# An encoder trunk on one core: the order at the start of a feed-forward stage, the place of a bias table's loads, and a last block turned back in two parts

## The chip, the core and the metric

The kernel runs on one core of a Trainium2 chip. Its engines each work through a queue of their own, in order: TensorE (PE: matmuls and transposes, with PEld for loading weights), VectorE (DVE), ScalarE (ACT), GpSimd (POOL), and SyncE (SP), which only issues DMAs. POOL issues DMAs too: those that add what they load to what is there. An instruction waits on semaphores for what it needs from other engines, and all that stands behind it in its queue waits with it.

The metric is the time of one execution in microseconds (us) on the device. One execution was also recorded by the profiler; the tables and rows come from it.

## The reference

A bidirectional encoder of two layers over 512 tokens of width 1024, all in float32. Each layer has a half-weighted SwiGLU feed-forward stage, a mixer, a second feed-forward stage, and a gated embedding (DEPTH is 2, the feed-forward width 2816):

```python
for i in range(DEPTH):
    h = h + 0.5 * swiglu(rmsnorm(h, norm_ffn1[i]), ffn1_w_gate[i], ffn1_w_up[i], ffn1_w_down[i])
    hn = rmsnorm(h, norm_mix[i])
    if i % 2 == 0:
        h = h + ab_mixer(hn, w_in_ab[j], sink_a[j], w_out_ab[j], pos)
    else:
        h = h + c_mixer(hn, w_in_c[j], rpb_c[j], w_out_c[j])
    h = h + 0.5 * swiglu(rmsnorm(h, norm_ffn2[i]), ffn2_w_gate[i], ffn2_w_up[i], ffn2_w_down[i])
    gate = jax.nn.sigmoid(rmsnorm(h, norm_ple[i]) @ w_ple_gate[i])
    h = h + gate * (p[i] @ w_ple_proj[i])
return rmsnorm(h, norm_final)

def swiglu(x, w_gate, w_up, w_down):
    return (jax.nn.silu(x @ w_gate) * (x @ w_up)) @ w_down
```

`c_mixer`, the mixer of the second layer, is a neighbourhood attention that adds a learned bias for each head and each offset in row and column, `rpb_c`.

## The kernel before

**Products.** A float32 operand is split into a high part, which ACT rounds off (L154), and the rest, which DVE subtracts (L155). Each product is three matmuls of these parts: high by high, high by low, low by high. So every weight that arrives passes ACT and then DVE before PE can use it. `wr` and `tmp` are raw weights, `wh` and `wl` their parts; `act` are activations and their parts.

**A feed-forward stage** (`ffn`) runs four times: two layers, two stages in each. It has four steps.
- `front` computes the first columns of gate and up as plain products over eight chunks of the input, into four PSUM banks, two called `mm` and two called `sc`. Meanwhile it computes the norm of each token (`stat`): PE sums up the squares, DVE makes the mean `ms` (L237), POOL raises it to the power -1/2 as `rcol` (L238). At the end DVE makes `minus`, which is minus `rcol` (L283), ACT applies Silu from each bank (L291) and DVE multiplies gate and up (L292), which reads the bank too. In the last four chunks, `halves` (L301 to L311) makes sums and differences of the input's quarters, for the blocks.
- `block` runs five times. Each multiplies a tile of 2 by 2 quarters by a scheme with seven products in place of eight, of 24 matmuls each. Its quarters of weights, q0 to q3, come in two ways: `whole` loads two units of 512 KB into `wr` on SP's queue (L329), and `add` lets a DMA on POOL's queue add another quarter to them (L335); `pieces` loads four units of 256 KB into `tmp` (L341), to which POOL's queue may add four more (L343). The first product uses the pieces of q3; the second uses `whole(q0)`, writes the `sc` banks, and thus waits until L291 and L292 have read what `front` left there; the third uses `whole(q2)`, the fourth the pieces of q1 and q2. L392 adds one whole quarter to another on DVE.
- `between` and `turn_back` transpose each block's result so that it can be the next operand: sixteen transposes of 128x128 on PE (L425), in groups of four into one bank, and one eviction by ACT for each group (L426). For the first four blocks this happens within the next block. For the last one, `turn` does it in `down`.
- `down` multiplies by the third matrix. It works in units of two chunks: `first(s)` splits the left halves of the activations (`x1`) and multiplies, `second(s)` splits the right ones (`x2`) and multiplies, `fifth` and the others follow. `turn()` is called once, behind `second(0)`; `first(1)` and `second(1)` come right behind it and split the two pairs of activations that `turn` appended. The four turns are at about 249, 880, 1273 and 1841 us.

**Order.** The code is written in one stream, and a scheduler orders each engine's queue from it, by what every step needs and by priorities: work inside `tc.high_priority()` goes first. `issue_after(x)` tells the scheduler to queue what is in it behind instruction x. The rest of the order comes out of the scheduler: which load stands before which on SP, or which split before which on DVE, is nowhere written out.

**Bias table.** `c` (the second layer's mixer) regroups `rpb` into a table in DRAM, `rpb_u`, by 32 DMAs of 15 KB from DRAM to DRAM (L1222). They depend on nothing, and the scheduler put them at the start of the program; the first reader runs at about 1404 us.

Of the kernel before, what the change touches and what calls it, by code (L numbers as in the profile page):

```python
# [13 lines left out]
ALU = mybir.AluOpType  # L14
# [42 lines left out]
class Trunk:  # L57
# [172 lines left out]
    def stat(self, tag, cols):  # L230
# [7 lines left out]
        nc.gpsimd.tensor_tensor(r[:, :n], ms[:, :n], self.mhalf[:, :n], op=ALU.pow)  # L238
# [27 lines left out]
    def front(self, w):  # L266
# [18 lines left out]
        for b in (2, 3, 0, 1):  # L285
# [4 lines left out]
            with self.tc.high_priority():  # L290
                nc.scalar.activation(g, banks[b][:, :M // 2], AF.Silu, scale=r)  # L291
                nc.vector.scalar_tensor_tensor(out[b], banks[b][:, M // 2:], r, g, op0=ALU.mult, op1=ALU.mult)  # L292
# [21 lines left out]
    def block(self, w, y, t, between, late):  # L314
# [10 lines left out]
        def whole(q):  # L325
            out = []
            for u in range(2):
                raw = self.wr.tile([P, UNIT], F32, tag="wr", name=self.nm("wr"))
                nc.sync.dma_start(raw, q[:, u * UNIT:(u + 1) * UNIT])  # L329
                out.append(raw)  # L330
# [6 lines left out]
        def pieces(q, more=None):  # L337
            out = []
            for k in range(half):
                raw = self.tmp()  # L340
                nc.sync.dma_start(raw, q[:, k * M:(k + 1) * M])  # L341
# [31 lines left out]
        chain = whole(q0)  # L373
# [8 lines left out]
        product(A, base, y[:half], l, True, False)  # L382
# [4 lines left out]
        product(C, pieces(q1, q2), t34, l, True, True)  # L387
# [31 lines left out]
    def turn_back(self, rows, bank):  # L419

        out = []
        for c in range(rows[0].shape[-1] // P):
# [7 lines left out]
    def ffn(self, i, which, k_next):  # L430
# [23 lines left out]
        for j in range(BLOCKS):  # L454
            n = 4 * UNIT + j * 8 * UNIT
            rows = self.block(gu[:, n:n + 8 * UNIT], y, t, between, late)
        self.begin_norm(k_next)
        p = lambda: [self.per_layer(i, c) for c in range(2)]
        self.down(dn, a, xs, sums, begin, kept, p if which == 2 else None, lambda: a.extend(self.turn_back(rows, self.sbank)))
# [16 lines left out]
    def down(self, w, a, xs, sums, begin, kept, inner, turn):  # L476
# [108 lines left out]
        for s in range(n):  # L585
            first(s)
            second(s)
            if s == 0:
                turn()
                r3 = [self.sbank(), self.sbank()]  # L590
# [610 lines left out]
    def c(self, k_next):  # L1201
# [15 lines left out]
        pad = io["rpb"]  # L1217
        nr = 2 * NA_KH - 1
        ud = self.dp.tile([NA_KW, 16, 2, nr, 16], F32, name="rpb_u")
        for c in range(NA_KW):  # L1220
            for g in range(2):
                nc.sync.dma_start(ud[c, :, g], bass.AP(tensor=pad.tensor, offset=pad.offset + NA_KW - 1 - c + 16 * g,  # L1222
                                                       ap=[[nr * RPB_W, 16], [RPB_W, nr], [1, 16]]))
        uh = ud.rearrange("c h g d r -> c (h g) (d r)")
# [65 lines left out]
        self.out_proj(io["o_c"], mix, KC - 2, k_next, self.kept)  # L1290

# [167 lines left out]
def encoder_trunk(ctx: ExitStack, tc: tile.TileContext, io: dict):  # L1459
    t = Trunk(ctx, tc, io)  # L1460
    t.setup()
    for i in range(DEPTH):
        t.ffn(i, 1, 4 * i + 1)
# [145 lines left out]
```

## Time and profile before

| | |
|---|---|
| time, median of three runs | 2020.44 us (2017.29, 2020.44, 2022.22) |
| time of the profiled execution | 2017.92 us |
| its span, first to last instruction | 2016.2 us |
| mean granted clock of TensorE | 0.996 of full speed |
| busy ACT | 1214.6 us (60% of the span), 2059 instructions |
| busy POOL | 342.3 us (17%), 398 instructions |
| read from HBM | 313.86 MB, 164 GB/s over the span |

The profile is one execution on the chip. A row of an engine in order of time gives the start in us from the span's start, the busy time, the engine, the line of the code, the operation with what it writes and reads, and how many like instructions in a row it holds; in brackets stands the time that the engine stood idle ahead of it, and what released it. PE's, DVE's and ACT's times are those of the engine's work; DMA issues on SP (SPq) give how long the queue was held. A stretch row gives the stretch, its length, then busy time of PE, PEld, DVE, ACT and POOL, the granted clock, the DMA share (over 1 when transfers queue up) and GB/s. The profile's span is what the engines worked; the time has 1.72 us around it.

### The profile page before, as it was taken

The page shows a single profiled execution, that of the slowest core. Times are in us where ns is not written, and L with a number is a line of the kernel's source. Part 1 is how long each engine was busy: PE and PEld are TensorE (multiplying, and loading weights), DVE is VectorE, ACT ScalarE, POOL GpSimd, SP SyncE. Part 2 cuts the span into 40 slices and gives each one's busy share as a digit, 9 for nine tenths or more (in the row PEclk, how much of TensorE's full clock was granted, in tenths as well). Part 3 has the DMA queues.
Part 4 walks back from the last instruction along what each step waited for, and adds up shares of the span by engine and source line. Part 5 has one row for each costly group of instructions (what it writes and reads, how often), then busy time and mean ns, then how long its engine had stood idle before and what let it go on. Part 6 is the DMA issues. An engine that isn't in the chain of part 4 may idle for free. (4 is left out here: it accounts for less than half of the span.)

```text
span 2016.2 us, 28073 instructions
## 1 busy us (share of the span) xinstructions
PE 1983.2 (98%) x9750; PEld 1652.0 (82%) x9750; DVE 1513.0 (75%) x2600; ACT 1214.6 (60%) x2059; POOL 342.3 (17%) x398
## 2 busy tenths in 40 slices
PE   8999999999999999999999999999999999999998
PEld 6888888878888888878888888788888888887886
DVE  7677876798766677786787678857887767778675
ACT  6655665477645665665566656745766566666553
POOL 1211011342211221112122120111000122111211
PEclk9999999999999999999999999999999999999999
DMA  9877687644335887779578786885343487776971
GB/s 271 185 194 184 151 198 202 185 94 85 89 74 186 194 195 174 173 177 213 195 229 183 169 186 174 191 195 183 105 131 106 161 205 185 170 172 177 216 229 43
DMA packets 150495, 344.05 MB, mean 171 GB/s; under 512 B 26320, under 2 KB 34000, under 8 KB 150352
## 3 DMA queue, kind: packets, MB, share of 16 engines
q1 hardware_dynamic: 109248, 227.89, 35.0%
q0 software_dynamic: 40960, 114.32, 32.3%
q8 instruction: 77, 1.26, 0.3%
q14 instruction: 66, 0.54, 0.1%
q10 hardware_dynamic: 144, 0.04, 0.0%
HBM read 313.86 MB, written 17.27 MB: 164 GB/s over the span
## 5 line engine op out<-in xcount | busy, mean ns | idle before, releaser
L154 ACT ACTIVATE wh<-wr 128x1024 fp32r<-128x1024 f32 (+1 forms) x408 | 419.1, 1029 | 434.0 <-PE mm L367 92.7
L155 DVE TENSOR_TENSOR wl<-wr,wh 128x1024 fp32r<-128x1024 f32 (+1 forms) x408 | 486.8, 1195 | 250.7 <-ACT wh L154 247.8
L365 PE MATMUL mm<-wh,act 128*128 128x512 f32 x640 | 250.7, 392 | 0.0
L367 PE MATMUL mm<-wh,act 128*128 128x512 f32 x640 | 250.6, 392 | 0.0
L366 PE MATMUL mm<-wl,act 128*128 128x512 f32 x640 | 249.3, 389 | 0.0
L154 ACT ACTIVATE wh<-tmp 128x512 fp32r<-128x512 f32 x280 | 165.7, 625 | 107.8 <-PE sc L367 32.7
L155 DVE TENSOR_TENSOR wl<-tmp,wh 128x512 fp32r<-128x512 f32 x280 | 181.8, 683 | 21.2 <-ACT wh L154 20.3
L179 PE MATMUL mm<-act,wh 128*128 128x512 f32 (+1 forms) x472 | 184.8, 393 | 0.4 <-ACT act L154 0.4
L181 PE MATMUL mm<-act,wl 128*128 128x512 f32 (+1 forms) x472 | 184.2, 391 | 0.0
L180 PE MATMUL mm<-act,wh 128*128 128x512 f32 (+1 forms) x472 | 184.1, 391 | 0.0
L335 POOL DMA_DIRECT2D wr<-in_gu_dram x80 | 78.8, 986 | 397.7 <-DVE wl L155 361.2
L366 PEld LDWEIGHTS mm<-wl,act 128*128 128x128 f32 x640 | 120.2, 188 | 24.5
L367 PEld LDWEIGHTS mm<-wh,act 128*128 128x128 f32 x640 | 120.2, 188 | 24.3
L365 PEld LDWEIGHTS mm<-wh,act 128*128 128x128 f32 x640 | 120.2, 188 | 23.7
L155 DVE TENSOR_TENSOR act<-act,act 128x512 fp32r<-128x512 f32 (+1 forms) x208 | 128.2, 638 | 9.5 <-ACT act L154 8.7
L365 PE MATMUL sc<-wh,act 128*128 128x512 f32 x320 | 125.4, 392 | 8.2 <-DVE act L292 8.2
L154 ACT ACTIVATE act<-act 128x512 fp32r<-128x512 f32 (+1 forms) x208 | 116.1, 588 | 26.9 <-PE sc L518 9.4
L508 POOL DMA_DIRECT2D wr<-in_dn_dram x80 | 69.4, 882 | 363.1 <-DVE wl L155 211.2
L367 PE MATMUL sc<-wh,act 128*128 128x512 f32 x320 | 125.3, 392 | 0.0
L366 PE MATMUL sc<-wl,act 128*128 128x512 f32 x320 | 125.2, 391 | 0.0
L343 POOL DMA_DIRECT2D tmp<-in_gu_dram x80 | 71.7, 1043 | 289.6 <-DVE act L473 134.3
L517 PE MATMUL mm<-wh,act 128*128 128x512 f32 x248 | 97.7, 394 | 5.4 <-ACT act L154 5.4
(271 smaller groups left out, 4562.3 us busy)
## 6 DMA issues: line engine op xcount, KB each, us to landing
wr<-in_gu_dram SPq DMA_DIRECT2D x92, 512.0 KB, 4.9
tmp<-in_gu_dram SPq DMA_DIRECT2D x160, 256.0 KB, 3.8
wr<-in_gu_dram POOLq DMA_DIRECT2D x80, 512.0 KB, 7.5
wr<-in_dn_dram POOLq DMA_DIRECT2D x64, 512.0 KB, 7.5
tmp<-in_dn_dram SPq DMA_DIRECT2D x120, 256.0 KB, 4.1
tmp<-in_gu_dram POOLq DMA_DIRECT2D x80, 256.0 KB, 5.9
wr<-in_dn_dram SPq DMA_DIRECT2D x32, 512.0 KB, 4.9
act<-kept SPq DMA_DIRECT2D x56, 256.0 KB, 4.6
```

The costliest lines, as they stand in the source:

```text
L154: self.put(self.nc.scalar.activation(hi, src, AF.Copy))
L155: self.put((lo_eng or self.nc.vector).tensor_tensor(lo, src, hi.bitcast(F32), op=ALU.subtract))
L179: mm(out, stat[0], mov[0], start=start, stop=False)
L180: mm(out, stat[0], mov[1], start=False, stop=False)
L181: return mm(out, stat[1], mov[0], start=False, stop=stop)
L335: nc.gpsimd.dma_start(raw, q[:, u * UNIT:(u + 1) * UNIT], accum_op=ALU.add)
L343: nc.gpsimd.dma_start(raw, more[:, k * M:(k + 1) * M], accum_op=ALU.add)
L365: mm(p, xh, wh, start=start and k == 0, stop=False, skip_group_check=True)
L366: mm(p, xh, wl, start=False, stop=False, skip_group_check=True)
L367: self.last_mm = mm(p, xl, wh, start=False, stop=stop and k == half - 1, skip_group_check=True)
L508: nc.gpsimd.dma_start(raw, b[:, u.start * T:u.stop * T], accum_op=ALU.add)
L517: mm(p, xh, wh, start=start and k == 0, stop=False, skip_group_check=True)
```

## The change

Four things change.

1. *The start of each feed-forward stage.* In every first to fifth block, the pieces of q1 and q2 and the DMAs that add to them are queued behind the last `power` (L238) that was issued. In the very first block of the program alone (`start`), two more: the loads of q0 are queued behind the last piece of q3 (`last_piece`), and the third product, with its splits, behind the last Silu of `front` (`last_silu`).
2. *The bias table* leaves `c` and becomes a function of its own, `bias_table`, called ahead of the second layer. Its DMAs are queued behind the last whole load (`last_load`) that was issued by then, which is one of the last block of the first layer's second feed-forward stage.
3. *The last block's turn* is made in two calls: the first two groups of four transposes behind `second(0)` as before, the other two behind `first(1)`.
4. `turn_back` takes the groups that it is to turn, and the Silu's, power's and loads' instructions are kept in names so that others can be queued behind them.

What is computed is the same.

```diff
+        self.power = nc.gpsimd.tensor_tensor(r[:, :n], ms[:, :n], self.mhalf[:, :n], op=ALU.pow)
...
+                self.last_silu = nc.scalar.activation(g, banks[b][:, :M // 2], AF.Silu, scale=r)
...
-    def block(self, w, y, t, between, late):
+    def block(self, w, y, t, between, late, start):
...
+                self.last_load = nc.sync.dma_start(raw, q[:, u * UNIT:(u + 1) * UNIT])
...
+                self.last_piece = nc.sync.dma_start(raw, q[:, k * M:(k + 1) * M])
...
         product(B, pieces(q3), y[half:], l, True, True)
-        chain = whole(q0)
+        with self.tc.issue_after(self.last_piece.ins) if start else ExitStack():
+            chain = whole(q0)
...
         base = whole(q2)
-        product(A, base, y[:half], l, True, False)
+        with self.tc.issue_after(self.last_silu.ins) if start else ExitStack():
+            product(A, base, y[:half], l, True, False)
...
-        product(C, pieces(q1, q2), t34, l, True, True)
+        with self.tc.issue_after(self.power.ins):
+            mixed = pieces(q1, q2)
+        product(C, mixed, t34, l, True, True)
...
-    def turn_back(self, rows, bank):
+    def turn_back(self, rows, bank, cs=None):
...
-        for c in range(rows[0].shape[-1] // P):
+        for c in cs or range(rows[0].shape[-1] // P):
...
-            rows = self.block(gu[:, n:n + 8 * UNIT], y, t, between, late)
+            rows = self.block(gu[:, n:n + 8 * UNIT], y, t, between, late, first and j == 0)
...
-        self.down(dn, a, xs, sums, begin, kept, p if which == 2 else None, lambda: a.extend(self.turn_back(rows, self.sbank)))
+        self.down(dn, a, xs, sums, begin, kept, p if which == 2 else None, lambda n: a.extend(self.turn_back(rows, self.sbank, n)))
...
         for s in range(n):
             first(s)
+            if s == 1:
+                turn(range(2, 4))
+                r3 = [self.sbank(), self.sbank()]
             second(s)
             if s == 0:
-                turn()
-                r3 = [self.sbank(), self.sbank()]
+                turn(range(2))
...
+    def bias_table(self):
...
+        with self.tc.issue_after(self.last_load.ins):
+            for c, g in ((c, g) for c in range(NA_KW) for g in range(2)):
+                self.nc.sync.dma_start(self.ud[c, :, g], bass.AP(tensor=pad.tensor, offset=pad.offset + NA_KW - 1 - c + 16 * g,
+                                                       ap=[[nr * RPB_W, 16], [RPB_W, nr], [1, 16]]))
...
     for i in range(DEPTH):
+        if i % 2:
+            t.bias_table()
         t.ffn(i, 1, 4 * i + 1)
```

How this moves the queues shows at three places. The rows give the line, the operation, what it writes and reads, and the shape; the lines of the new kernel are some higher (L380 was L379, L396 was L392, L430 was L426).

SP's queue at the start of the program, behind the loads of the input and of `front`'s weights. `ident` and `sink` are small constants, `wr` the whole quarters q0 (473, 475) and q2 (529, 531), `tmp` 429 to 435 the pieces of q3. Before:

```order
L147 DMA ident<-in_ident_dram 128x128
L329 DMA wr_473<-in_gu_dram 128x1024
L329 DMA wr_475<-in_gu_dram 128x1024
L907 DMA sink_3269<-in_sink_dram 128x12
L1222 DMA rpb_u<-in_rpb_dram 16x15x16 x2
L329 DMA wr_529<-in_gu_dram 128x1024
L1222 DMA rpb_u<-in_rpb_dram 16x15x16 x3
L329 DMA wr_531<-in_gu_dram 128x1024
L1222 DMA rpb_u<-in_rpb_dram 16x15x16
L341 DMA tmp_429<-in_gu_dram 128x512
L341 DMA tmp_431<-in_gu_dram 128x512
```

Now:

```order
L147 DMA ident<-in_ident_dram 128x128
L913 DMA sink_3269<-in_sink_dram 128x12
L341 DMA tmp_429<-in_gu_dram 128x512
L341 DMA tmp_431<-in_gu_dram 128x512
L341 DMA tmp_433<-in_gu_dram 128x512
L341 DMA tmp_435<-in_gu_dram 128x512
L329 DMA wr_473<-in_gu_dram 128x1024
L329 DMA wr_475<-in_gu_dram 128x1024
L329 DMA wr_529<-in_gu_dram 128x1024
L329 DMA wr_531<-in_gu_dram 128x1024
```

The four pieces of q3 moved from behind four whole loads and six DMAs of the table to a place ahead of all of them; the table is gone from here. It is now in the same queue in the last block of the first layer's second feed-forward stage, in groups of 6, 15, 1 and 10 between the loads of `down`'s weights.

DVE's queue from `minus` to the first L292, the multiplication that frees the `sc` banks. `wl_534` and `wl_538` are splits of q2, `wr_529` under L392 the sum of two quarters. Before:

```order
L283 TENSOR_SCALAR minus_403<-rcol_322 128x4
L155 TENSOR_TENSOR act_370<-act_360,act_369 128x512
L155 TENSOR_TENSOR wl_534<-wr_529,wh_533 128x1024
L308 TENSOR_TENSOR act_389<-act_385 128x256
L310 TENSOR_TENSOR act_390<-act_387,act_385 128x256
L309 SCALAR_TENSOR_TENSOR act_389<-act_389,act_387 128x256
L392 TENSOR_TENSOR wr_529<-wr_529,wr_473 128x1024
L311 SCALAR_TENSOR_TENSOR act_390<-act_389,act_387 128x256
L155 TENSOR_TENSOR act_396<-act_389,act_395 128x512
L155 TENSOR_TENSOR wl_538<-wr_531,wh_537 128x1024
L155 TENSOR_TENSOR act_400<-act_390,act_399 128x512
L292 SCALAR_TENSOR_TENSOR act_405<-sc_224,rcol_322,act_406 128x256
```

Now the same stretch, up to the first row behind the four L292:

```order
L155 TENSOR_TENSOR act_370<-act_360,act_369 128x512
L308 TENSOR_TENSOR act_389<-act_385 128x256
L309 SCALAR_TENSOR_TENSOR act_389<-act_389,act_387 128x256
L310 TENSOR_TENSOR act_390<-act_387,act_385 128x256
L311 SCALAR_TENSOR_TENSOR act_390<-act_389,act_387 128x256
L155 TENSOR_TENSOR act_396<-act_389,act_395 128x512
L155 TENSOR_TENSOR act_400<-act_390,act_399 128x512
L292 SCALAR_TENSOR_TENSOR act_405<-sc_224,rcol_322,act_406 128x256
L292 SCALAR_TENSOR_TENSOR act_405<-sc_225,rcol_322,act_406 128x256
L292 SCALAR_TENSOR_TENSOR act_411<-mm_222,rcol_322,act_412 128x256
L292 SCALAR_TENSOR_TENSOR act_411<-mm_223,rcol_322,act_412 128x256
L155 TENSOR_TENSOR wl_534<-wr_529,wh_533 128x1024
```

The two splits and the sum of quarters that stood ahead of L292 stand behind it. `minus` has left this stretch as well; it now stands further ahead, between the last L311 of the second half and the split of the fourth piece of q3:

```order
L308 TENSOR_TENSOR act_329<-act_325 128x256
L237 TENSOR_SCALAR ms_321<-tr_316 128x4
L309 SCALAR_TENSOR_TENSOR act_329<-act_329,act_327 128x256
L310 TENSOR_TENSOR act_330<-act_327,act_325 128x256
L311 SCALAR_TENSOR_TENSOR act_330<-act_329,act_327 128x256
L283 TENSOR_SCALAR minus_403<-rcol_322 128x4
L155 TENSOR_TENSOR wl_444<-tmp_435,wh_443 128x512
L155 TENSOR_TENSOR act_336<-act_329,act_335 128x512
```

It reads `rcol`, which POOL's L238 writes; in POOL's queue the power stood behind one adding DMA in the first block and now stands ahead of it. In the first blocks of the three other feed-forward stages three to six adding DMAs change places with the power in the same way.

ACT's queue at the first turn. `act_2236` to `act_2257` (before) and `act_2236` to `act_2284` (now) are the evictions of the four groups of transposes, the rows with `act_1192`, `act_1522`, `act_1199` and `act_1529` are the splits of the activations for `first(1)` and `second(1)`, `wh_2361` the split of a weight. Before:

```order
L154 ACTIVATE wh_2361<-tmp_2363 128x512
L426 ACTIVATE act_2236<-sc_2235 128x512
L426 ACTIVATE act_2243<-sc_2242 128x512
L154 ACTIVATE wh_2361<-tmp_2364 128x512
L426 ACTIVATE act_2250<-sc_2249 128x512
L426 ACTIVATE act_2257<-sc_2256 128x512
L154 ACTIVATE act_2267<-act_1192 128x512
L154 ACTIVATE act_2271<-act_1522 128x512
L154 ACTIVATE act_2292<-act_1199 128x512
```

Now:

```order
L154 ACTIVATE wh_2361<-tmp_2363 128x512
L430 ACTIVATE act_2236<-sc_2235 128x512
L430 ACTIVATE act_2243<-sc_2242 128x512
L154 ACTIVATE act_2251<-act_1192 128x512
L154 ACTIVATE wh_2361<-tmp_2364 128x512
L154 ACTIVATE act_2255<-act_1522 128x512
L430 ACTIVATE act_2277<-sc_2276 128x512
L430 ACTIVATE act_2284<-sc_2283 128x512
L154 ACTIVATE act_2292<-act_1199 128x512
```

The split of `act_1192`, which the first product behind the turn needs, stood behind all four evictions and stands behind two now. On PE nothing changes places: the sixteen transposes still follow each other, and the products of `first(1)` come behind them.

More of the change, by code (lines that the diff above doesn't have):

```diff
@@ L237, in stat @@
         nc.vector.tensor_scalar(ms[:, :n], ps[:, :n], 1.0 / D, EPS, op0=ALU.mult, op1=ALU.add)
-        nc.gpsimd.tensor_tensor(r[:, :n], ms[:, :n], self.mhalf[:, :n], op=ALU.pow)
+        self.power = nc.gpsimd.tensor_tensor(r[:, :n], ms[:, :n], self.mhalf[:, :n], op=ALU.pow)
         return r
@@ L290, in front @@
             with self.tc.high_priority():
-                nc.scalar.activation(g, banks[b][:, :M // 2], AF.Silu, scale=r)
+                self.last_silu = nc.scalar.activation(g, banks[b][:, :M // 2], AF.Silu, scale=r)
                 nc.vector.scalar_tensor_tensor(out[b], banks[b][:, M // 2:], r, g, op0=ALU.mult, op1=ALU.mult)
@@ L328, in whole @@
                 raw = self.wr.tile([P, UNIT], F32, tag="wr", name=self.nm("wr"))
-                nc.sync.dma_start(raw, q[:, u * UNIT:(u + 1) * UNIT])
+                self.last_load = nc.sync.dma_start(raw, q[:, u * UNIT:(u + 1) * UNIT])
                 out.append(raw)
@@ L340, in pieces @@
                 raw = self.tmp()
-                nc.sync.dma_start(raw, q[:, k * M:(k + 1) * M])
+                self.last_piece = nc.sync.dma_start(raw, q[:, k * M:(k + 1) * M])
                 if more is not None:
@@ L1215, in constants @@
                         nc.scalar.activation(dst[i][hf][free, :], t[free, :], AF.Copy)
[L1217 to L1224, printed above, removed]
+        uh = self.ud.rearrange("c h g d r -> c (h g) (d r)")
         nat = lambda x, b: x[:, b * P:(b + 1) * P]
@@ L1290, in c @@
         self.out_proj(io["o_c"], mix, KC - 2, k_next, self.kept)
+    def bias_table(self):
+        pad = self.io["rpb"]
+        nr = 2 * NA_KH - 1
+        self.ud = self.dp.tile([NA_KW, 16, 2, nr, 16], F32, name="rpb_u")
+        with self.tc.issue_after(self.last_load.ins):
+            for c, g in ((c, g) for c in range(NA_KW) for g in range(2)):
+                self.nc.sync.dma_start(self.ud[c, :, g], bass.AP(tensor=pad.tensor, offset=pad.offset + NA_KW - 1 - c + 16 * g,
+                                                       ap=[[nr * RPB_W, 16], [RPB_W, nr], [1, 16]]))
     @staticmethod
```

## The prediction

> **What bounds the kernel now.** I read the page's first part, then the busy time in stretches of 20 us, then the order of time of each engine where a stretch is not full.
>
> ```profile
> PE 1983.2 (98%) x9750; PEld 1652.0 (82%) x9750; DVE 1513.0 (75%) x2600; ACT 1214.6 (60%) x2059; POOL 342.3 (17%) x398
> ...
> 20.00:40.00 20.00, 14.24 (x67) 11.59 (x65) 17.73 (x36) 14.18 (x22) 8.72 (x9) 0.99 1.08 303
> 40.00:60.00 20.00, 17.58 (x73) 14.52 (x74) 10.90 (x16) 11.10 (x20) 3.56 (x5) 0.84 0.94 168
> ...
> 240.00:260.00 20.00, 18.26 (x88) 14.84 (x87) 16.80 (x27) 14.42 (x25) 2.60 (x3) 1.00 0.70 164
> ...
> 880.00:900.00 20.00, 18.26 (x86) 14.67 (x85) 17.42 (x30) 16.16 (x28) 2.32 (x3) 1.00 0.82 190
> ...
> 1260.00:1280.00 20.00, 18.26 (x88) 14.87 (x87) 18.14 (x30) 15.04 (x26) 2.59 (x3) 1.00 0.74 175
> ...
> 1840.00:1860.00 20.00, 18.26 (x81) 14.50 (x80) 15.29 (x26) 14.64 (x25) 2.60 (x3) 0.91 0.75 180
> ```
>
> TensorE works 1983.2 of 2016.2 us: only its 33 us of idle time, and stretches at a lower clock, can be won. The columns are the stretch, its length, busy PE, PEld, DVE, ACT and POOL, the granted clock, the DMA share and GB/s. In the first block 8.2 us are idle; in each of four other stretches exactly 1.74 us. Those four are the turns of the last block. The rest of the idle time lies where the change does not reach. So the change is worth what it takes from these five holes.
>
> **The first block, the hole.** PE in order of time:
>
> ```profile
> 33.63 0.39 PE L366 MATMUL ob<-wl,act 128*128 128x512 f32 x1
> 33.86 0.39 PE L367 MATMUL ob<-wh,act 128*128 128x512 f32 x1
> 42.42 0.77 PE L365 MATMUL sc<-wh,act 128*128 128x512 f32 x1 [8.17 <-DVE act L292]
> ```
>
> The first product ends at 34.25. The next one writes the two `sc` banks that `front` used, and L292 must read them first. L292 sits at the end of a queue on DVE that began late:
>
> ```profile
> 18.52 1.32 ACT L301 ACTIVATE act<-act,gain 128x512 f32<-128x512 f32 x2
> 23.43 0.63 ACT L154 ACTIVATE wh<-tmp 128x512 fp32r<-128x512 f32 x1 [3.59 <-DMA tmp<-in_gu_dram]
> ...
> 10.52 0.33 SPq L147 DMA_DIRECT2D ident<-in_ident_dram  x1
> 11.20 1.07 SPq L329 DMA_DIRECT2D wr<-in_gu_dram  x2
> ...
> 19.06 7.52 SPq L341 DMA_DIRECT2D tmp<-in_gu_dram  x12
> ...
> 29.57 20.07 SPq L1222 DMA_DIRECT2D rpb_u<-in_rpb_dram  x21
> ...
> tmp<-in_gu_dram SPq DMA_DIRECT2D x18, 256.0 KB, 5.3
> ```
>
> ACT had nothing to do for 3.59 us, because SP issued the pieces of the first quarter (`tmp`) at 19.06 only, behind four `wr` loads and six pieces of the bias table. In the new queue they stand behind `ident` and `sink`: the first goes out at about 11.9, the fourth some 2.1 us later at SP's pace there of 0.68 (10.52 to 11.20). With 5.3 us to landing (last row, the median of the first 60 us) they are there from 17.2 to 19.3. ACT is free for them at 19.7. So the load is no longer what DVE waits for:
>
> ```profile
> 21.62 0.42 DVE L311 SCALAR_TENSOR_TENSOR act<-act,act 128x256 f32<-128x256 f32 x1
> ...
> 24.10 0.69 DVE L155 TENSOR_TENSOR wl<-tmp,wh 128x512 fp32r<-128x512 f32 x1 [1.98 <-ACT wh L154]
> ...
> 27.34 0.16 DVE L237 TENSOR_SCALAR ms<-tr 128x4 f32<-128x4 f32 x1
> ...
> 35.71 1.22 DVE L155 TENSOR_TENSOR wl<-wr,wh 128x1024 fp32r<-128x1024 f32 x1
> ...
> 37.98 1.22 DVE L392 TENSOR_TENSOR wr<-wr,wr 128x1024 f32<-128x1024 f32 x1
> ...
> 41.80 0.87 DVE L292 SCALAR_TENSOR_TENSOR act<-sc,rcol,act 128x256 f32<-128x256 f32 x2
> ```
>
> From 24.10 to 41.80 DVE is all but full, so each part of that queue counts:
> - It starts at 22.0, where L311 ends, and not at 24.10: 2.1 us less.
> - Two splits `wl<-wr` (35.71 is one) and one L392 move behind L292: three times 1.22, which overlap a little, 3.4 us less.
> - A wait is added. `minus` (L283) now stands right behind L311 of the second half, and needs the power, which takes this long:
>
> ```profile
> 28.32 1.72 POOL L238 TENSOR_TENSOR rcol<-ms,mhalf 128x4 f32<-128x4 f32 x1
> ```
>
> `ms` comes out at about 25.4 in the new order, so the power ends at 27.2 at the earliest, where DVE would be at 26.4: about 1.0 us more. Behind `minus` on DVE stand the split of the fourth piece and all of the chain to L292; PE waits for L292 alone, since the fourth piece is due at 32.7 on PE. The power itself, moved ahead of an adding transfer on POOL, gives nothing more: L291 is not at its place on ACT before 36.
>
> L292 comes at 41.80 - 2.1 - 3.4 + 1.0 = 37.3, and PE follows it by the 0.62 of today (41.80 to 42.42) at 37.9. The hole is 3.7 us in place of 8.17: **4.5 us less**. The bounds: if the pieces land no earlier than today, 2.1 us of it are lost (2.4); if the added wait is nothing, 1.0 more (5.5). What is late next: the splits moved behind L292 are due when PE has done the 24 matmuls of this product and the eight transposes behind it, 6 us later, and take some 4 us. They are covered.
>
> **The first block, the clock.**
>
> ```profile
> 35.00:40.00 5.00, 0.00 (x0) 0.00 (x0) 4.95 (x10) 3.22 (x5) 5.00 (x6) 0.95 1.14 197
> 40.00:45.00 5.00, 2.58 (x6) 2.15 (x7) 4.58 (x8) 2.64 (x7) 0.10 (x1) 0.50 1.24 205
> 45.00:50.00 5.00, 5.00 (x21) 3.98 (x21) 1.29 (x2) 1.15 (x2) 0.00 (x0) 0.87 0.72 95
> ```
>
> After the hole the clock is 0.50 until 46.3 (0.87 over the last stretch is 1.3 us at half). Of it PE works from 42.42, 3.9 us, and loses half: **1.9 us**. The clock fell at about 39.5 (0.95 over the first), that is 5.2 us after the last matmul; the shorter hole ends before that. I take the whole 1.9 us; the bound is nothing gained.
>
> The Trainium skill (TensorE: Matmul & The Clock Gate, Part 1: The HAM clock gate) states that an idle window of about 3.4 us, which runs free of the program, halves the clock, and advises against PE gaps over some 3 us; by it a hole of 3.7 us is still long enough in some executions, and the sum would be 1.6 us worse there. The rows above agree in that the fall came within the hole, not at its start.
>
> **The four turns.** Transposes, their evictions on ACT, and the next product, at the first of the four:
>
> ```profile
> 250.29 1.15 PE L425 MATMUL sc<-ident,act 128*128 128x128 f32 x8 [0.38 <-ACT act L426]
> 252.79 0.50 PE L517 MATMUL mm<-wh,act 128*128 128x512 f32 x1 [1.35 <-ACT act L154]
> ...
> 249.66 1.07 ACT L426 ACTIVATE act<-sc 128x512 f32<-128x512 f32 x2
> 250.61 0.63 ACT L154 ACTIVATE wh<-tmp 128x512 fp32r<-128x512 f32 x1
> 251.13 1.09 ACT L426 ACTIVATE act<-sc 128x512 f32<-128x512 f32 x2
> 252.09 2.21 ACT L154 ACTIVATE act<-act 128x512 fp32r<-128x512 f32 x4
> ...
> 250.76 0.42 DVE L471 TENSOR_TENSOR act<-act,act 128x256 f32<-128x256 f32 x1 [0.28 <-ACT act L426]
> ```
>
> PE is done with its transposes at 251.44 and waits 1.35 us for the split of `x1` at 252.09, which ACT does behind all four evictions. In the new queue of ACT that split stands third, behind two evictions, at the place of 250.61: done at 251.24, before the transposes end. PE's own order does not change here: the sixteen transposes still stand together, so the 0.38 stays. What is late next is the low half of the split on DVE, behind L471: 251.2 to 251.9, due four matmuls (0.23 each, 33.63 to 33.86) after 251.44, at 252.4. This is close, and so are the next splits, so I keep 0.1 us back: 4 x 1.25 = **5.0 us**, between 0 (another wait in its place) and 5.4.
>
> At the fourth turn the clock fell as well:
>
> ```profile
> 1844.00:1846.00 2.00, 1.48 (x5) 1.19 (x6) 1.91 (x4) 2.00 (x5) 0.00 (x0) 0.78 1.06 236
> 1846.00:1848.00 2.00, 2.00 (x6) 1.58 (x5) 2.00 (x5) 1.52 (x4) 0.00 (x0) 0.50 1.03 264
> 1848.00:1850.00 2.00, 2.00 (x9) 1.60 (x8) 0.27 (x1) 0.78 (x1) 0.00 (x0) 0.87 0.35 130
> ```
>
> 0.9, 2.0 and 0.5 us at half clock are 3.4 us, of which half is lost: 1.7 us, all of it PE's. The 20-us rows of the other three turns show 1.00. With the 1.35 us gone I expect no such fall: **1.7 us** in the profiled execution, nothing in one that had no fall.
>
> **The bias table and the other blocks cost nothing.**
>
> ```profile
> L1222 SPq DMA_DIRECT2D rpb_u<-in_rpb_dram x32: 532/606/2115, 13.2 to 55.0; - x32
> ...
> 852.26 5.77 SPq L492 DMA_DIRECT2D wr<-in_dn_dram  x3
> ...
> 871.71 1.04 ACT L154 ACTIVATE wh<-wr 128x1024 fp32r<-128x1024 f32 x1
> ```
>
> The 32 pieces go, in groups of 6, 15, 1 and 10, onto SP's queue in the last block of the second FFN, from about 818. At the 0.96 us of the row at 29.57 (20.07 for 21) they hold SP 31 us, with some ten loads between them to about 854. The load now issued at 852.26 is used at 871.71. It lands about 859, 13 us early; that cover is gone only at 1.4 us a piece. Table readers come some 550 us later. In the first blocks of the other three FFNs the power goes ahead of three to six adding transfers on POOL; PE has no idle row in those stretches, and the transfers have a product (5.4 us) of cover, so nothing there, between 0 and 1 us each.
>
> **Sum.** 4.5 + 1.9 + 5.0 + 1.7 = 13.1. The profiled execution took 2017.92 us (span 2016.2 and 1.72 around it): 2004.8. The median of the three runs, 2020.44, is 2.5 us above it; from it, without the fourth turn's clock, 2020.44 - 11.4 = 2009.0. I say **2006**.
>
> **Rivals.**
> - *The clock falls in the short hole too.* For it: at the fourth turn PE stood still for only 0.38 and 1.35 us, with transposes between, and the clock fell. Against it: three equal turns show 1.00. Then 1.9 us stay: 2008.
> - *The queue on DVE starts as late as now*, because the pieces land late under the load of the DMA (share 1.08 in the stretch 20 to 40). Against it: they have 2.5 us to spare. 2.1 us, and the clock with it: 2010.
> - *The split in two parts does nothing*, as the transposes keep their order on PE and another wait, the low half on DVE, ends as late as the old one. Against it: the margin of 0.5 us above. 5.0 and 1.7 us stay: 2012.7.
> - *The whole does nothing that shows:* each hole is taken by the next wait: 2016 to 2020.
> - *Slower: the table holds up SP before the `dn` loads.* It decides from 1.4 us a piece. At the longest piece now, 2.1 us, SP is held 67 us, the load lands at 895, 23 us late, PE stands for about 20: 2026. For it: one piece did take 2.115. Against it: the median is 0.606.
>
> **Chances.** Forecast 52, clock 18, late pieces 11, turns 8, nothing 6, slower 5 in 100. The range of 2000 to 2013 holds the first four but for the rims, and reaches down for executions that lie as far below the profiled one as it lies below the median, with both upper bounds (5.5 and 5.4). About 0.3%, 6 us, is what a measurement of this kernel can tell from no change: faster 0.87, same 0.08, slower 0.05.
>
> **What would show it.** Right: PE's hole at 34.25 ends near 37.9 on L292 with no 0.50 stretch behind it, ACT starts on `tmp` at 19.7, DVE has a wait of about 1 us on POOL at L283; at the turns a wait of 0.38 and none of 1.35; no idle PE from 840 to 880. Wrong: ACT still waits for a DMA there, L283 holds DVE for longer, a new PE wait on DVE's L155 behind the transposes, or on a `wr` load near 872.

## The result and the profile after

| | before | after |
|---|---|---|
| median of five runs each | 2019.4 us (2016.66 to 2022.22) | 2008.96 us (2005.45 to 2009.9) |
| ratio of the times | | 0.9946 (95%: 0.9932 to 0.9961) |
| time of the profiled execution | 2017.92 us | 2009.9 us |
| its span | 2016.2 us | 2008.0 us |

The change makes the kernel 10.4 us (0.5%) faster. 2006 us had been forecast, within 2000 to 2013; that is 13.4 us below this median of the kernel before, and 14.4 us below the median of the three runs that were known then. Two later executions, one each of two kernels of the experiments, took 2820 and 7045 us; they are left out of every time and ratio below.

First the page's first part and the stretches with the first block, the first turn and the fourth turn (length, busy PE, PEld, DVE, ACT and POOL, granted clock, DMA share, GB/s), now of the changed kernel:

```profile
PE 1983.9 (99%) x9750; PEld 1651.7 (82%) x9750; DVE 1510.9 (75%) x2600; ACT 1212.0 (60%) x2059; POOL 341.9 (17%) x398
...
20.00:40.00 20.00, 16.57 (x74) 13.50 (x73) 19.36 (x42) 16.27 (x28) 8.56 (x9) 0.94 0.99 295
40.00:60.00 20.00, 20.00 (x84) 16.36 (x83) 12.06 (x13) 11.39 (x17) 3.48 (x4) 0.89 0.96 189
240.00:260.00 20.00, 19.62 (x93) 15.90 (x93) 17.70 (x29) 14.76 (x25) 3.97 (x5) 1.00 0.84 196
1840.00:1860.00 20.00, 20.00 (x89) 16.39 (x88) 18.72 (x32) 13.82 (x22) 3.46 (x4) 1.00 0.86 210
```

TensorE's work is the same; its idle time is what shrank. The first turn's stretch (240 to 260) holds 0.38 us of idle time where it held 1.74, and at the fourth turn the clock is 1.00 where it was 0.91. But 0.94 and 0.89 say that the clock still falls in the first block.

PE in order of time there, and the queue on DVE that it waits for:

```profile
34.80 0.39 PE L367 MATMUL ob<-wh,act 128*128 128x512 f32 x1
38.61 0.76 PE L365 MATMUL sc<-wh,act 128*128 128x512 f32 x1 [3.43 <-DVE act L292]
```

```profile
22.89 0.42 DVE L311 SCALAR_TENSOR_TENSOR act<-act,act 128x256 f32<-128x256 f32 x1
23.23 0.69 DVE L155 TENSOR_TENSOR wl<-tmp,wh 128x512 fp32r<-128x512 f32 x1
...
28.09 0.17 DVE L283 TENSOR_SCALAR minus<-rcol 128x4 f32<-128x4 f32 x1 [0.23 <-POOL rcol L238]
...
37.99 0.87 DVE L292 SCALAR_TENSOR_TENSOR act<-sc,rcol,act 128x256 f32<-128x256 f32 x2
```

The hole is 3.43 us in place of 8.17. DVE goes from L311 to the first piece without a wait, and waits 0.23 us for the power at L283. SP now issues the four pieces from 12.92 on, and ACT takes the first as soon as it is free:

```profile
12.92 2.40 SPq L341 DMA_DIRECT2D tmp<-in_gu_dram  x4
```

```profile
21.02 0.61 ACT L154 ACTIVATE wh<-tmp 128x512 fp32r<-128x512 f32 x1
```

Cut into stretches, the same place shows what the clock did:

```profile
35.20:37.60 2.40, 0.00 (x0) 0.00 (x0) 2.27 (x6) 1.51 (x3) 2.40 (x4) 1.00 1.05 194
37.60:38.60 1.00, 0.00 (x0) 0.02 (x1) 1.00 (x3) 1.00 (x4) 0.95 (x2) 0.50 1.12 205
38.60:44.40 5.80, 5.79 (x14) 4.54 (x15) 4.63 (x6) 3.31 (x6) 0.00 (x0) 0.50 1.10 208
44.40:46.00 1.60, 1.60 (x9) 1.29 (x8) 1.18 (x2) 0.91 (x2) 0.00 (x0) 1.00 1.13 206
```

It fell 2.4 us after the last matmul and stayed at half for 6.8 us, of which TensorE worked 5.8. Before, it fell 5.2 us after the last matmul, and TensorE worked 3.9 us at half.

The first turn, PE and then ACT:

```profile
247.38 1.15 PE L429 MATMUL sc<-ident,act 128*128 128x128 f32 x8 [0.38 <-ACT act L430]
248.38 0.50 PE L521 MATMUL mm<-wh,act 128*128 128x512 f32 x1
```

```profile
246.75 1.07 ACT L430 ACTIVATE act<-sc 128x512 f32<-128x512 f32 x2
247.70 0.63 ACT L154 ACTIVATE act<-act 128x512 fp32r<-128x512 f32 x1
```

The split runs behind two evictions and ends at 248.33, just ahead of the product at 248.38, which waits for nothing. (One sentence in the description of the kernel is wrong: `first(1)` and `second(1)` split results of earlier blocks, such as `act_1192`, and not what `turn` appended. That is used by later units, so `first(1)` waited for the turn's evictions only because ACT's queue held them ahead of its split.)

PE's waits in total (time, times, longest), the three longest groups in the part that the change touches:

```profile
PE sc L365 <- DVE act L292: 3.4, 1, 3.4
PE mm L366 <- DVE wl L155: 1.7, 2, 1.0
PE sc L429 <- ACT act L430: 1.5, 4, 0.4
```

The second line is new: two waits for a split of `wr`, of which this is the longer:

```profile
703.13 0.50 PE L366 MATMUL mm<-wl,act 128*128 128x512 f32 x1 [0.98 <-DVE wl L155]
```

```profile
695.90 1.06 ACT L154 ACTIVATE wh<-wr 128x1024 fp32r<-128x1024 f32 x1 [6.43 <-DMA wr<-in_gu_dram]
```

And the start of the program, before and after, differs without any help from the change:

```profile
5.71 0.81 PE L179 MATMUL mm<-wh,act 128*128 128x512 f32 x2
```

```profile
6.08 1.19 PE L179 MATMUL mm<-wh,act 128*128 128x512 f32 x2
```

TensorE's early matmuls took the short time of 0.39 to 0.40 us from 6.35 on before, and from 7.11 on after; by the end of the first product the execution after was 0.94 us behind (33.86 and 34.80 for the same matmul). Over all the profiles of this document the first L180 starts between 6.24 and 7.18 us, the earliest in a kernel (power_start) that has the changed kernel's queues there, so this is a matter of the execution.

### The profile page after: what moved, and what is told of

It is laid out like the page before. It is cut to its first block, busy times and chain, and to the rows that moved or that the text cites. A ratio compares the mean times of both kernels' runs of the same rounds, so it can differ in the third digit from the quotient of the medians.

```text
span 2008.0 us, 28069 instructions
## 1 busy us (share of the span) xinstructions
PE 1983.9 (99%) x9750; PEld 1651.7 (82%) x9750; DVE 1510.9 (75%) x2600; ACT 1212.0 (60%) x2059; POOL 341.9 (17%) x398
## 4 chain that ended last, share of the span: by engine, by line
PE 72%; DVE 4%; ACT 2%; DMA 2%; issue 1%; POOL 0%; DVEq 0%; ACTq 0%; POOLq 0%
PE mm L366 5%; PE mm L367 5%; PE mm L365 5%; PE mm L179 5%; PE mm L180 5%; PE mm L181 5%; PE sc L367 2%; PE sc L366 2%; PE sc L365 2%; PE mm L521 2%; PE mm L523 2%; PE mm L522 2%; PE sc L523 2%; PE sc L522 1%; PE sc L521 1%; DMA wr<-in_gu_dram 1%
## 5 line engine op out<-in xcount | busy, mean ns | idle before, releaser
L365 PE MATMUL mm<-wh,act 128*128 128x512 f32 x640 | 250.7, 392 | 0.0
L367 PE MATMUL mm<-wh,act 128*128 128x512 f32 x640 | 250.6, 392 | 0.0
L155 DVE TENSOR_TENSOR wl<-tmp,wh 128x512 fp32r<-128x512 f32 x280 | 182.0, 686 | 14.4 <-ACT wh L154 14.1
L180 PE MATMUL mm<-act,wh 128*128 128x512 f32 (+1 forms) x472 | 184.2, 391 | 0.0
L396 DVE TENSOR_TENSOR wr<-wr,wr 128x1024 f32<-128x1024 f32 x40 | 49.0, 1225 | 77.7 <-DMA wr<-in_gu_dram 77.7
```

The lines of the kernel that those rows point to most:

```text
L155: self.put((lo_eng or self.nc.vector).tensor_tensor(lo, src, hi.bitcast(F32), op=ALU.subtract))
L180: mm(out, stat[0], mov[1], start=False, stop=False)
L365: mm(p, xh, wh, start=start and k == 0, stop=False, skip_group_check=True)
L367: self.last_mm = mm(p, xl, wh, start=False, stop=stop and k == half - 1, skip_group_check=True)
```

## The experiments

Every ratio is to the kernel before, run on the same chip in turns, and has its 95% interval behind it.

**The turn alone.** The kernel before with the parts of the diff on `turn_back`, on `ffn`'s last line and on `down`:

```diff
             first(s)
+            if s == 1:
+                turn(range(2, 4))
+                r3 = [self.sbank(), self.sbank()]
             second(s)
             if s == 0:
-                turn()
-                r3 = [self.sbank(), self.sbank()]
+                turn(range(2))
```

> The kernel before with the turn in two parts and nothing else. My account: at each of the four turns the wait of 1.35 us on ACT's split goes and the one of 0.38 us stays, with no new wait on DVE's low half, so 5.4 us less idle time on TensorE; the first block keeps its hole of 8.2 us. About 2014 us against 2019.4, ratio 0.997; up to 1.7 us less again where an execution of the kernel before loses clock at a turn. Rival: another wait takes the place of the old one at the turns, ratio 1.000, and most of the gain of the whole change comes from the first block.

Ratio 0.9972 (0.9961 to 0.9983), 2012.32 us. PE's longest waits:

```profile
PE sc L365 <- DVE act L292: 8.1, 1, 8.1
PE tr L1441 <- ACT tmp L1435: 1.7, 1, 1.7
PE sc L425 <- ACT act L426: 1.5, 4, 0.4
```

The four waits of 1.35 us are gone, and 0.38 each is left. Half of the whole gain is the turn's: 5.7 us by the ratio, for 5.4 us of waits.

**The splits moved behind the Silu.** The changed kernel without that part:

```diff
-        with self.tc.issue_after(self.last_silu.ins) if start else ExitStack():
-            product(A, base, y[:half], l, True, False)
+        product(A, base, y[:half], l, True, False)
```

> The changed kernel without the third product's splits queued behind the last Silu: two splits of wr and one sum of quarters stand ahead of L292 on DVE again. My account: three times 1.22 us, overlapping a little, 3.4 us more ahead of L292, so the hole in the first block is 6.8 us in place of 3.43, and the whole 3.4 us slower. Rival: DVE waits for ACT there anyway (idle gaps of 1.3 us on ACT), and the hole grows by less than 1.5 us.

The hole is 5.69 us, ratio 0.9960 (0.9945 to 0.9975): 2.3 us more, between the two expectations. On DVE the way from the third chunk's L311 to L292 took 8.6 us (31.11 to 39.73) where it takes 5.6 in the changed kernel (32.39 to 37.99): the edit is worth 3.0 us there. The other 0.7 us is how this execution's DVE stood against its PE ahead of that stretch: its L311 ran 3.2 us ahead of PE's last matmul of the first product (34.28), the changed kernel's 2.4 us (34.80).

**The order of the loads, and the table.** First q0's loads let ahead of q3's pieces again; then, in another kernel, the table's loads put back into `c`:

```diff
-        with self.tc.issue_after(self.last_piece.ins) if start else ExitStack():
-            chain = whole(q0)
+        chain = whole(q0)
```

> The changed kernel without q0's loads queued behind the pieces of q3: the pieces are issued behind the four whole loads, with no table pieces between. The step of the prediction gave 2.1 us to the earlier pieces as a whole. By SP's pace now (0.57 to 0.6 us a load) the pieces go out 2.3 us later, from about 15.2 to 17, and land from 20 to 23 us; ACT takes the first at 21.0 and the others from 23.2. My account: the departure of the bias table did this work, and the order of q3 against q0 and q2 adds 0 to 0.7 us: hole 3.4 to 4.1 us. Rival: the order is what counts, the hole is 5.5 us or more.

```diff
+        pad = io["rpb"]
...
+        ud = self.dp.tile([NA_KW, 16, 2, nr, 16], F32, name="rpb_u")
+        for c in range(NA_KW):
+            for g in range(2):
+                nc.sync.dma_start(ud[c, :, g], bass.AP(tensor=pad.tensor, offset=pad.offset + NA_KW - 1 - c + 16 * g,
+                                                       ap=[[nr * RPB_W, 16], [RPB_W, nr], [1, 16]]))
...
     for i in range(DEPTH):
-        if i % 2:
-            t.bias_table()
```

> The changed kernel with the bias table's loads in their old place in the code. The order of the queues then has fourteen of them on SP ahead of the pieces of q3. My account: at SP's pace of 0.6 to 0.65 us these hold the pieces back by 9 us, from 12.9 to about 22; they land from 26 us, DVE's queue in the first block starts 4 to 5 us late, and the hole is 7.5 to 9 us, as long as before the change: the start's gain hangs on the table's move. About 4 to 5.5 us slower than the changed kernel, ratio to the kernel before 0.997. Rival: small loads from DRAM to DRAM cost SP little and the hole stays under 5 us.

Without q3 first the hole is 3.66 us and the ratio 0.9949 (0.9935 to 0.9964): ACT waits for the first piece, and DVE a little for ACT:

```profile
22.18 0.63 ACT L154 ACTIVATE wh<-tmp 128x512 fp32r<-128x512 f32 x1 [2.03 <-DMA tmp<-in_gu_dram]
```

```profile
22.85 0.69 DVE L155 TENSOR_TENSOR wl<-tmp,wh 128x512 fp32r<-128x512 f32 x1 [0.55 <-ACT wh L154]
```

With the table back the hole is 6.24 us, the ratio 0.9965 (0.9954 to 0.9977). SP's queue and ACT in that kernel:

```profile
12.11 9.10 SPq L1228 DMA_DIRECT2D rpb_u<-in_rpb_dram  x14
21.25 3.01 SPq L341 DMA_DIRECT2D tmp<-in_gu_dram  x4
```

```profile
25.10 0.63 ACT L154 ACTIVATE wh<-tmp 128x512 fp32r<-128x512 f32 x1 [5.17 <-DMA tmp<-in_gu_dram]
```

Fourteen loads of 15 KB hold the queue 9.1 us, and the hole is between the two expectations. So of the two edits that bring the first quarter earlier, the table's move does the work (2.8 us of hole). But that is more than the change gained by it: the kernel before had six of these loads ahead of the pieces and issued them at 19.06, this one at 21.25. What the order of the quarters adds can't be told: 0.2 us of hole, where two profiles of the changed kernel itself differ by 0.8.

**The clock.** Twelve idle matmuls between the first two products, in a bank that nobody reads:

```diff
         product(B, pieces(q3), y[half:], l, True, True)
+        if start:
+            idle = self.tbank()
+            for _ in range(12):
+                nc.tensor.matmul(idle, y[half][0][:, :P], y[half][0], start=True, stop=True, skip_group_check=True)
```

> The changed kernel with twelve idle matmuls (128x512, 0.23 us each, 2.7 us together) put on TensorE between the first and the second product of the first block, into a bank nobody reads; all other queues are the same. The second product can start no earlier, since it waits for L292. My account: the clock falls at the end of a window of 3.41 us in which TensorE worked less than about 0.4 of the time, and rises after a window that is full; the hole of 3.43 us makes such a window in most executions, and TensorE then works 2.8 to 5.7 us at half clock. With the hole filled up to 0.7 us the clock stays at 1.00 behind it, and 1.4 to 2.85 us are won: ratio to the kernel before 0.9935 to 0.994. Rival: the fall has to do with something else (the power drawn when all engines work, or the switch between fp32r products and others), and the 0.50 stretch stays; ratio 0.9946 as for the changed kernel.

Ratio 0.9932 (0.9917 to 0.9947), 2003.29 us. PE, and two stretches:

```profile
34.09 2.88 PE L376 MATMUL tr<-act 128*128 128x512 f32 x12
37.45 0.47 PE L365 MATMUL sc<-wh,act 128*128 128x512 f32 x1 [0.48 <-DVE act L292]
```

```profile
35.00:40.00 5.00, 4.52 (x20) 3.47 (x19) 4.79 (x10) 4.96 (x10) 2.41 (x3) 1.00 1.11 204
40.00:45.00 5.00, 5.00 (x27) 4.22 (x27) 5.00 (x6) 3.41 (x7) 0.00 (x0) 1.00 1.09 204
```

Counted from the end of the first product, the second starts hardly sooner, 3.20 us behind it (34.25 and 37.45) where the hole was 3.43, but at full clock (0.47 for its first matmul, where the changed kernel has 0.76). That is nearly the whole difference in this block; from 35 to 40 us DVE and ACT are no less busy than in the changed kernel (4.79 and 4.96 us against 4.73 and 3.91), so the fall hangs on PE's idle time and not on the load of the others. The changed kernel run again:

> The changed kernel once more, for a second profile. By my account of the clock: the hole of 3.4 us is there again, and in this execution it either makes a window with TensorE less than about 0.4 busy (in some seven of ten executions), and the clock falls for 3.4 or 6.8 us, or it is split evenly between two windows and the clock stays at 1.00. By account A a wait on a split of wr in a later stage with a chance of about one half. Ratio to the kernel before 0.9946 within 0.001.

Ratio 0.9938 (0.9921 to 0.9954), 2005.61 us. Its profile has a hole of 2.65 us, none of the waits for `wr`, and the clock fell again, for half as long:

```profile
33.00:35.00 2.00, 1.61 (x8) 1.00 (x6) 1.90 (x6) 0.66 (x2) 2.00 (x5) 1.00 1.00 190
35.00:40.00 5.00, 2.74 (x7) 2.19 (x8) 4.80 (x9) 4.96 (x10) 2.21 (x3) 0.68 1.13 209
40.00:45.00 5.00, 5.00 (x27) 4.19 (x26) 4.48 (x5) 2.01 (x4) 0.00 (x0) 0.98 1.09 203
```

**The power ahead of the adding DMAs in the later stages.** Only POOL's queue differs here:

```diff
-        with self.tc.issue_after(self.power.ins):
+        with self.tc.issue_after(self.power.ins) if start else ExitStack():
             mixed = pieces(q1, q2)
```

> The changed kernel, but the adding DMAs are queued behind the norm's power in the first feed-forward stage only; in the other three the power stands behind three to six of them, as before. Only POOL's queue differs from the changed kernel. My account: the two waits of TensorE on a split of wr that the changed kernel has and the kernel before does not (0.98 us at 703, 0.69 us at 1096) come from the adding DMAs being held back and bunched, and go: 1.7 us less idle time, ratio to the kernel before about 0.994 where the changed kernel has 0.9946. Rival 1: they come from the stream being earlier or from the load of the DMA, and stay, of about the same size. Rival 2: the late power costs TensorE time at L291 and L292 of the later stages: new waits of up to 1 us each.

Ratio 0.9939 (0.9922 to 0.9955), 2005.91 us, and both waits are gone; no new wait of PE appears in the later stages. The same pair was made with the idle matmuls:

> The twelve idle matmuls, with the adding DMAs behind the power in the first stage alone; only POOL's queue differs from the run with twelve idle matmuls. By account A no wait on a split of wr in a later stage, by account B one with a chance of about four in ten. In both the clock stays at 1.00 in the first block, and the ratio to the kernel before is 0.9925 to 0.9935.

Ratio 0.9924 (0.9910 to 0.9939), 2003.48 us; no such wait, and clock 1.00 in the first block. Its partner, with the power ahead in all stages, had none either, and 2003.29 us. The count over all profiles follows behind the next pair.

**The evictions of `front` first.** In the first stage alone, the sums of the third and fourth chunk are queued behind L292:

```diff
-        t = []
+        t, start = [], bool(self.ahead)
...
-            if k >= KC // 2:
+            if k >= KC // 2 and (k < KC - 2 or not start):
                 t.append(self.halves(k - KC // 2))
...
-                nc.vector.scalar_tensor_tensor(out[b], banks[b][:, M // 2:], r, g, op0=ALU.mult, op1=ALU.mult)
+                last = nc.vector.scalar_tensor_tensor(out[b], banks[b][:, M // 2:], r, g, op0=ALU.mult, op1=ALU.mult)
+        if start:
+            with self.tc.issue_after(last.ins):
+                t += [self.halves(c) for c in range(KC // 2 - 2, KC // 2)]
```

> The changed kernel with the sums of the third and fourth chunk (L301 to L311) and their splits queued behind L292 in the first stage, so that the banks are read as soon as front is done. My account: L292 is held up by DVE's queue alone; L291 and L292 then run from about 30 to 32.5 us, before the first product ends at 35.2; the hole of 3.43 us goes, the clock does not fall, and the second product's third and fourth chunk are split in time (needed 2.7 and 4.1 us after 35.2) or up to 1.5 us late: 4 to 6 us less than the changed kernel, ratio to the kernel before 0.9916 to 0.9926. Rival: the work that is put off is only late for the second product, whose waits then take back 3 us or more: ratio 0.994 or above.

Ratio 0.9924 (0.9908 to 0.9941), 2003.7 us. No hole is left ahead of the second product, the clock stays at 1.00, and 0.84 us comes back later:

```profile
40.70 0.50 PE L368 MATMUL sc<-wh,act 128*128 128x512 f32 x1 [0.84 <-ACT act L154]
```

ACT had taken three splits of weights for the third and fourth product ahead of the fourth chunk's, and the split that PE waits for had to wait itself for DVE:

```profile
40.01 0.63 ACT L154 ACTIVATE act<-act 128x512 fp32r<-128x512 f32 x1 [0.84 <-DVE act L314]
```

The sums of the fourth chunk (the last, L314, at 39.56) stood on DVE behind two splits and the sum of two quarters for the third product (34.55, 36.29 and 38.43). So in the next two kernels the third product's splits are queued behind that chunk's last split (`self.last_silu = self.last_split`, kept by `split`). They differ from each other by the power's place alone, which is in the first stage only in the first of them:

> The evictions of front first, as in the run before, with the third product's splits queued behind the last split of the fourth chunk, and the adding DMAs queued behind the power in the first stage alone. My account: the wait of 0.84 us at 40.7 in the run with the evictions first came from three splits of weights ahead of the fourth chunk's on ACT; it falls to 0.4 us or less, the clock stays at 1.00 in the first block, and no wait on a split of wr is left in the later stages: ratio to the kernel before 0.991 to 0.992, faster than the changed kernel by 5 us or more. Rival: what is moved behind is late for the third product in its turn, and the ratio stays at 0.9924 or above.

> The same with the adding DMAs behind the power in all four stages, as in the changed kernel; only POOL's queue differs. So far waits of PE on a split of wr in the first or second block of a later stage, 0.4 to 1.8 us each, showed in four of seven profiles of kernels with the adding DMAs behind the power in all stages, and in none of three with them ahead of it. Account A: the order on POOL makes them, by chance of the DMA: this profile has one or more of them with a chance of about one half, its partner has none, and its median is 0 to 1.5 us above its partner's. Account B: chance alone: its partner has them as often.

Ratios 0.9913 (0.9898 to 0.9928), 2001.51 us, and 0.9914 (0.9899 to 0.9929), 2001.6 us. Neither has a wait from the first product to the first turn; the first of them:

```profile
31.71 0.47 DVE L292 SCALAR_TENSOR_TENSOR act<-sc,rcol,act 128x256 f32<-128x256 f32 x1
```

```profile
35.00:40.00 5.00, 5.00 (x23) 4.02 (x23) 4.61 (x9) 3.62 (x7) 2.90 (x4) 1.00 1.11 199
40.00:45.00 5.00, 5.00 (x28) 4.24 (x26) 4.24 (x6) 5.00 (x10) 0.00 (x0) 1.00 1.10 209
```

These two beat both kernels: 17.5 us below the kernel before, and 4 to 7 us below the two medians of the changed one.

On the waits for `wr`: in all profiles together, those with the power ahead in every stage show them in four of nine (after, table_back, evict, turn_pe), the others in none of five. By their ratios the three pairs alike but for POOL differ by 0.0007, 0.0008 and 0.0001 (0.2 to 1.6 us) in favour of the power ahead in the first stage alone, and the changed kernel run again stands 0.0001 the other way; each ratio is known to about 0.0015. Whether POOL's order makes these waits or chance does is open. That in table_back two of the four came in the first stage (72 and 77 us), where every kernel with the change has the same order on POOL, speaks for chance, or for the table's loads.

**The 0.38 us left at each turn.** The second half of the transposes is queued behind the product of `first(1)`:

```diff
             if s == 1:
-                turn(range(2, 4))
+                with self.tc.issue_after(marks[1].ins):
+                    turn(range(2, 4))
```

> The changed kernel with the second half of the turn's transposes queued behind the product of first(1), so that the sixteen transposes no longer stand together on TensorE. My account: the 0.38 us that is left at each of the four turns comes from the ninth transpose waiting for ACT to empty a bank; with a product between, it goes, 1.5 us in all, ratio 0.7 thousandths below that of the changed kernel (too little to time, to be read in the profile). Rival: first(1) stands closer to its splits then, and a wait for them of 0.4 us or more takes its place.

The waits of the rival came: ratio 0.9984 (0.9975 to 0.9993), 2015.2 us, 6 us or more above the changed kernel. The waits at the first turn:

```profile
246.49 0.50 PE L521 MATMUL mm<-wh,act 128*128 128x512 f32 x1 [1.39 <-ACT act L154]
...
251.21 0.98 PE L521 MATMUL sc<-wh,act 128*128 128x512 f32 x2 [0.81 <-ACT act L430]
```

The second eight transposes were the cover under which ACT evicts and splits for `first(1)`. With them moved, PE meets the same wait that the change had removed, and another for the last evictions. The 0.38 us is the cheaper way.

## Why the prediction was right, and where it was wrong

The terms, as forecast and as the two profiled executions show them (the one of the changed kernel was the slowest of its five runs):

| term | forecast | measured |
|---|---|---|
| hole of the first block | 4.5 | 4.7 (8.17 to 3.43) |
| its clock | 1.9 | -0.9 (work at half clock 3.9 to 5.8 us, half of it lost) |
| the four turns | 5.0 | 5.4 |
| clock at the fourth turn | 1.7 | 1.7 |
| other blocks | 0 | -1.7 (0.98 and 0.69) |
| start of the program | none | -0.9 |
| sum | 13.1 | 8.3; the spans differ by 8.2 |

- **What bounds the kernel, and the turns**: right. TensorE's busy time is the same within 0.7 us, and the gain is mostly idle time of the five holes (10.1 us of it, against losses elsewhere). The turn alone gives the forecast's 5.0 with 5.4; the 0.1 us kept back at each turn was not needed, since the low half on DVE was not late.
- **The hole**: right, with small errors that cancel (the same kernel's two profiles have 3.43 and 2.65 us, so a part of a microsecond is chance). The splits moved behind L292 were put at 3.4 us; taking that edit back costs DVE 3.0. The wait added at L283 was put at 1.0 us; it is 0.23, since the power took 1.25 us in place of 1.72 and DVE reached L283 later. The earlier load was put at 2.1 us; DVE's first split of a piece came 9.8 us ahead of the first product's last matmul before (24.10 and 33.86) and 11.6 after (23.23 and 34.80), that is 1.8. From that split to L292 DVE took 17.7 us before and 14.8 after, 2.9 less; the two make up the 4.7. Most of the earlier load is the table's move, and not q3 ahead of q0, by the two experiments; the forecast had not parted the two.
- **The clock of the first block**: the step that failed. "The clock fell at about 39.5, that is 5.2 us after the last matmul; the shorter hole ends before that" took 5.2 us for a delay that every hole has to last. In the changed kernel the fall came 2.4 us after the last matmul. The first rival named this outcome at 2008, 18 in 100; there 1.9 us were to stay as they are, and in the profiled execution the loss grew to 2.9. With the idle matmuls the loss is gone, while the second product still starts 3.2 us behind the first.
- The Trainium skill (TensorE: Matmul & The Clock Gate, Part 1: The HAM clock gate) puts the fall at the end of an idle window of about 3.4 us that runs free of the program. The stretches at half clock here last 3.4 or 6.8 us, which agrees. But TensorE need not be idle for a whole window: the clock fell with holes of 3.43 and 2.65 us, and in the turn_pe profile behind a single wait of 1.78. The section's rule as the prediction weighed it named the right outcome, and its 1.6 us on the sum would have been nearer.
- **Bias table at its new place**: right that it is free there. SP spent 24.0 us on it (3.89, 12.15, 0.54 and 7.43 for the four groups), less than the 31 reckoned with, and PE shows no wait between 840 and the turn. **Slower** did not come near.
- **Other blocks at nothing**: the profiled execution has 1.7 us of waits against it, others have none; see the experiments.
- **The time**: the sum gave 2004.8 from the profiled execution and 2009.0 from the median, and the forecast took 2006 between them without naming a reason. 2008.96 came out; the miss of 3 us is about the size of the clock's term, but also of what two sets of runs of the changed kernel differ by (2008.96 and 2005.61). The second profile's span is 13.1 us below that of the kernel before, just the forecast's sum, and that is luck: its hole gave 5.5 us in place of 4.5, its clock 0.5 in place of 1.9, and it had no wait on `wr`.

## What to carry to other kernels

Where an engine's wait ends on a queue, ask first what in that queue the waiter does not need: earlier loads and fewer splits took the hole from 8.2 to 3.4 us, and two chunks' sums put behind the eviction took the rest. A hole of TensorE costs its length and, in every profile here with a hole of 2.6 us or more, half of the next 3 to 6 us of work; twelve idle matmuls in it took that second cost away where the first stayed. Before work is taken out of a place where it seems to make a wait, see what waits under its cover.

## What the runs showed of the hardware

- The clock can fall behind a wait far shorter than the 5.2 us of the forecast, and need not. In the turn_pe profile, a later block with one wait of 1.78 us:

```profile
1664.00:1667.00 3.00, 1.22 (x6) 0.70 (x5) 3.00 (x5) 3.00 (x7) 0.00 (x0) 1.00 0.07 27
1667.00:1670.50 3.50, 3.50 (x10) 2.73 (x9) 3.50 (x6) 1.05 (x2) 0.00 (x0) 0.51 0.86 266
1670.50:1672.00 1.50, 1.50 (x8) 1.21 (x7) 1.50 (x3) 1.18 (x2) 0.62 (x1) 1.00 0.81 275
```

  In the 3.41 us ahead of that fall (1663.65 to 1667.06) TensorE worked 1.63, so the account in the expectation of the idle matmuls, less than about 0.4 of a window, was set too low. In table_back a wait that was no shorter left the clock at 1.00:

```profile
76.79 0.50 PE L366 MATMUL mm<-wl,act 128*128 128x512 f32 x1 [1.84 <-DVE wl L155]
```

```profile
76.80:80.30 3.50, 3.50 (x15) 2.88 (x16) 3.50 (x7) 0.98 (x2) 0.00 (x0) 1.00 0.71 227
```

  Waits of 0.84 us (evict) and 0.48 us (fill12) did not do it either. In each of the five profiles with a hole of 2.6 to 3.7 us in the first block (after, after_again, power_start, no_q3, turn_pe) the clock fell, for 3.4 or 6.8 us. The length of the hole does not set which: 5.69 us (no_silu) had 3.4, and 8.1 and 8.17 us (turn_only, before) had 6.8.
- When TensorE's matmuls first take their short time differs by 0.8 us (6.35 and 7.11) between two executions with the same queues up to there. The granted clock in the rows of that stretch reads 1.00 in both, so these profiles do not show why. This and the length of the low clock may be a part of the 4 us by which runs of the changed kernel differ (2005.45 to 2009.9), which no run shows by itself; the two kernels without a fall in the first block and without a wait there agree within 0.8 us (2001.04 to 2001.87) and 2.3 us (2000.59 to 2002.91).
- Loads of 15 KB hold SP's queue 0.65 us each at the program's start (14 in 9.10, table_back), about as long as loads of 256 KB (0.60 in the changed kernel, four in 2.40, and 0.75 in table_back, four in 3.01).
